# Masked softmax of variable length on one Trainium2 core: 64-byte writes beside the first loads taken out, stores of seven batches cut in halves

## The chip, the core and the metric

The kernel runs on one core of a Trainium2 chip. The time is device microseconds from launch to the end of the program, as the median of three runs. The profile is one execution of the same program; its span, from the first instruction to the last, is about 1.65 us shorter than the time of the run.

A core has engines that work side by side: VectorE (DVE), ScalarE (ACT), GpSimd (POOL), TensorE (PE) and SyncE (SP). Transfers between the chip's main memory (HBM) and the on-chip memory (SBUF, 128 partitions) are carried by 16 DMA engines. An engine's program only issues a transfer; the transfer raises a semaphore when it has landed, and other engines wait for that semaphore.

## The reference

`x` is 16 batches of 8 heads of 256 x 256 numbers in fp32, and `lengths` holds one length for each batch. Each row gets a softmax over its first `length` columns, and zeros behind it:

```python
for b in range(batch):
    length = lengths[b]
    masked = x[b, :, :, :length]
    masked = masked - np.max(masked, axis=-1, keepdims=True)
    exp_masked = np.exp(masked)
    result[b, :, :, :length] = exp_masked / np.sum(exp_masked, axis=-1, keepdims=True)
```

One batch is 2048 rows of 1 KB, that is 2.097 MB. The lengths of this case, in order of batch, are 188, 233, 229, 243, 195, 252, 165, 210, 222, 180, 209, 157, 159, 199, 214 and 248. All 16 batches are written whole, 33.6 MB.

## The kernel before

A batch is one tile of 128 partitions, 16 rows of 256 numbers in each, so 16 KB in a partition. There are eight places (`slots`) for such tiles in SBUF. Half a batch is 8 rows (8 KB) in each partition, a quarter is 4 rows (4 KB).

**Loads.** SyncE issues the loads of batches 0 to 3 at once (batch 0 in two halves). GpSimd issues those of batches 4 to 15. It picks a width of 160 to 240 columns, or all 256, by the batch's length, and has two loads in flight: before it issues load `n` it waits for load `n-2` to have landed and for the store of batch `n-8` to be done.

```python
for h in range(2):
    s = slice(h * half, (h + 1) * half)
    nc.sync.dma_start(out=xt[:, 0, s], in_=x_f[0, :, s]).then_inc(s_ld[h], 16)
for b in range(1, ahead):                                   # ahead = 4
    nc.sync.dma_start(out=xt[:, b], in_=x_f[b]).then_inc(s_ld[b + 1], 16)
...
with nc.Fori(0, (batch - ahead) // 2, 1, engines=[POOL]) as q:
    for par in range(2):
        n = 2 * q + (ahead + par)
        v_len = length(POOL, word[0:1, bass.ds(2 * n, 1)])
        with nc.gpsimd.If(q >= 1):
            nc.gpsimd.wait_ge(s_sw[par], 16 * q)            # load n-2 has landed
            nc.gpsimd.wait_ge(s_st[par], 64 * q)            # store n-8 is done
        pick(v_len, bass.ds(n, 1), bass.ds(n % slots, 1), par, widths + [seq_k])
```

**The small writes.** Ahead of the loads ScalarE's own queue gets one transfer of 640 pieces of 64 bytes (16 x 40). It writes zeros into the place of the last batch in the output, which that batch's own store overwrites at the end.

```python
nc.vector.memset(touch, 0.0).then_inc(s_zero, 1)            # 16 x 40 x 16 numbers
nc.scalar.wait_ge(s_zero, 1)
out_e = out_f[batch - 1].rearrange("(e r) t k -> e (r t) k", e=16)[:, :often, :few]
nc.scalar.dma_start(out=out_e, in_=touch).then_inc(s_touch, 16)
```

**Compute.** VectorE masks a batch in place (`mask`), ScalarE takes the exponential of its 16 rows in each partition with their sums, and VectorE divides each half (`divide`). VectorE masks batch `b+1` before it divides batch `b`:

```python
for b in range(batch):
    if b == 0:
        divide(0, 0)
    if b + 1 < batch:
        mask(b + 1, slice(0, nt))       # waits for load b+1
    if b > 0:
        divide(b, 0)
    divide(b, 1)
```

**Stores.** SyncE issues them, on the queue on which it issued the first loads. How a batch is cut depends on its number: batch 0 whole, 1 to 9 in a half and two quarters, 10 and 11 in halves, 12 to 14 whole, 15 in halves. A piece waits until its half is divided; the first piece of batch `b` also waits until the store of batch `b-2` is done.

```python
def parts(b):
    if b == 0:
        cuts = [0, nt]
    elif b < 10:
        cuts = [0, half, half + quarter, nt]
    elif b < 12 or b == batch - 1:
        cuts = [0, half, nt]
    else:
        cuts = [0, nt]
    return [slice(i, j) for i, j in zip(cuts, cuts[1:])]
...
for b in range(batch):
    s_b = s_st[b % 2]
    for s in parts(b):
        nc.sync.wait_ge(s_out, 2 * b + (s.stop - 1) // half + 1)
        if b == batch - 1 and s.start == 0:
            nc.sync.wait_ge(s_touch, 16)
        if b >= 2 and s.start == 0:
            nc.sync.wait_ge(s_b, 64 * (b // 2 + 1))
        nc.sync.dma_start(
            out=out_f[b, :, s, :], in_=xt[:, b % slots, s, :]
        ).then_inc(s_b, 16 * ((s.stop - s.start) // quarter))
```

Of the kernel before, what the change touches and what calls it, by code (L numbers as in the profile page):

```python
# [9 lines left out]
F32 = mybir.dt.float32  # L10
# [10 lines left out]
def kernel(  # L21
# [6 lines left out]
    nc = tc.nc  # L28
    P = nc.NUM_PARTITIONS

    batch, heads, seq_q, seq_k = x.shape
# [7 lines left out]
    out_f = out.rearrange("b h q k -> b (h q) k").rearrange("b (p t) k -> b p t k", p=P)  # L39
# [10 lines left out]
    def parts(b):  # L50


        if b == 0:
            cuts = [0, nt]
        elif b < 10:
            cuts = [0, half, half + quarter, nt]
        elif b < 12 or b == batch - 1:
            cuts = [0, half, nt]
        else:
            cuts = [0, nt]  # L60
        return [slice(i, j) for i, j in zip(cuts, cuts[1:])]

    pool = ctx.enter_context(tc.tile_pool(name="all", bufs=1))
# [10 lines left out]
    row_sum = pool.tile([P, batch, nt], F32, name="row_sum")  # L74
    inv_sum = pool.tile([P, batch, nt], F32, name="inv_sum")
    warm = pool.tile([P, 1], F32, name="warm")
    few = 16
    often = 40
    touch = pool.tile([16, often, few], F32, name="touch")
    seed = pool.tile([1, 2], F32, name="seed")  # L80

    with tc.tile_critical(no_gpsimd_drain=True):  # L82
        sem = lambda n: ctx.enter_context(nc.semaphore(n))
        s_word = sem("s_word")
        s_ones = sem("s_ones")
        s_touch = sem("s_touch")
        s_zero = sem("s_zero")
        s_lenb = sem("s_lenb")
        s_lenf = sem("s_lenf")
        s_ld = [sem(f"s_ld{k}") for k in range(ahead + 1)]  # L90
# [18 lines left out]


        nc.scalar.dma_start(out=word64, in_=lengths[None, :]).then_inc(s_word, 16)


        nc.vector.memset(touch, 0.0).then_inc(s_zero, 1)  # L114
        nc.scalar.wait_ge(s_zero, 1)
        out_e = out_f[batch - 1].rearrange("(e r) t k -> e (r t) k", e=16)[:, :often, :few]
        nc.scalar.dma_start(out=out_e, in_=touch).then_inc(s_touch, 16)
        for h in range(2):
            s = slice(h * half, (h + 1) * half)
            nc.sync.dma_start(out=xt[:, 0, s], in_=x_f[0, :, s]).then_inc(s_ld[h], 16)  # L120
# [2 lines left out]
        for b in range(batch):  # L123
            s_b = s_st[b % 2]
            for s in parts(b):
                nc.sync.wait_ge(s_out, 2 * b + (s.stop - 1) // half + 1)
                if b == batch - 1 and s.start == 0:
                    nc.sync.wait_ge(s_touch, 16)
                if b >= 2 and s.start == 0:
                    nc.sync.wait_ge(s_b, 64 * (b // 2 + 1))  # L130
                nc.sync.dma_start(  # L131
                    out=out_f[b, :, s, :], in_=xt[:, b % slots, s, :]
                ).then_inc(s_b, 16 * ((s.stop - s.start) // quarter))
# [49 lines left out]
        def step(ins):  # L183
# [8 lines left out]
                out=down, in0=iota_i, scalar1=0.5, scalar2=-big, op0=ALU.add, op1=ALU.mult  # L192
# [7 lines left out]
                out=len_s, in0=len_f, scalar1=big, scalar2=None, op0=ALU.mult  # L200
# [56 lines left out]
        with nc.Fori(0, 2 * batch, 1, engines=[ACT]) as i:  # L257
            nc.scalar.wait_ge(s_min, i + 1)
            at = bass.ds(i % (2 * slots), 1)
            for j in range(half):  # L260
                e = x_h[:, at, j, :]
                ins = nc.scalar.activation(  # L262
                    out=e, in_=e, func=EXP, accum_out=sum_h[:, bass.ds(i, 1), j]
# [32 lines left out]
```

The softmax here doesn't subtract the row's maximum and nothing guards it: scores larger than these inputs give would overflow.

## Time and profile before

| What | Value |
|---|---|
| time, median of 3 (lowest to highest) | 156.48 us (156.45 to 156.49) |
| span of the profiled execution | 154.8 us |
| VectorE busy | 115.6 us, 75% |
| ScalarE busy | 105.2 us, 68% |
| bytes moved by DMA | 62.12 MB, 401 GB/s over the span |
| HBM read, written | 28.51 MB, 33.60 MB |
| stores issued | 18 of 512 KB, 15 of 1024 KB, 4 of 2048 KB |
| the transfer of 64-byte pieces, issue to landing | 28.0 us |

How to read it: the busy share of an engine is an average over the span. The page names the DMA queues by number: q1 is the one that SyncE issues to, q0 GpSimd's, q10 ScalarE's. A queue's share is the time that its packets took, summed over the 16 DMA engines, divided by 16 times the span or the stretch asked for. The chain of work that ended last is followed back from the end of the last compute instruction.

### The profile page before, as it was taken

The numbers are of one execution on the slowest core, as the hardware profiler recorded it, in microseconds if no ns is written. First come the engines' busy times: TensorE is split into PE (matmuls) and PEld (weight loads), VectorE is DVE, ScalarE is ACT, GpSimd is POOL, SyncE is SP. The second block draws the span as 40 slices with busy tenths as digits, with TensorE's granted clock in tenths as the row PEclk, the third lists the DMA queues.
The fourth block names the chain that finished last, engine by engine and source line by source line (L and its number), as shares of the span: only waits on it lengthen the run. The fifth ranks groups of instructions, "written<-read, shape, count | busy, mean of one in ns | idle before, by whom it ended". The sixth has DMA issues, their size and how long they took to land.

```text
span 154.8 us, 1319 instructions
## 1 busy us (share of the span) xinstructions
PE 0.2 (0%) x1; PEld 0.1 (0%) x1; DVE 115.6 (75%) x85; ACT 105.2 (68%) x514; POOL 19.0 (12%) x25
## 2 busy tenths in 40 slices
PE   0000000000000000000000000000000000000000
PEld 0000000000000000000000000000000000000000
DVE  2339999953999993986979499999894999990000
ACT  3097799992698897393978849798979397920000
POOL 4910031000220200202020020202000000000000
DMA  4999999999999999999999999999999999999993
GB/s 110 425 442 421 425 353 405 405 412 439 418 406 390 417 407 421 410 413 415 405 424 407 411 419 401 415 406 413 416 411 448 417 423 425 442 436 428 425 417 127
DMA packets 10788, 62.12 MB, mean 401 GB/s; under 512 B 1522, under 2 KB 1618, under 8 KB 7458
## 3 DMA queue, kind: packets, MB, share of 16 engines
q1 hardware_dynamic: 6048, 41.95, 65.9%
q0 software_dynamic: 4080, 20.12, 32.1%
q10 hardware_dynamic: 658, 0.04, 0.3%
q14 instruction: 2, 0.02, 0.0%
HBM read 28.51 MB, written 33.60 MB: 401 GB/s over the span
## 4 chain that ended last, share of the span: by engine, by line
DMA 71%; DVE 12%; issue 3%; SPq 2%; POOLq 1%; DVEq 0%
DMA xt<-in_x_dram 39%; DMA out_dram<-xt 32%; DVE xt L235 9%; DVE xt L208 3%; SPq L131 1%; SPq L120 1%; DVE inv_sum L232 0%; POOLq L104 0%; POOLq L143 0%; SPq L122 0%; POOLq L148 0%; POOLq L166 0%; DVEq L225 0%; POOLq L170 0%; POOLq L150 0%
## 5 line engine op out<-in xcount | busy, mean ns | idle before, releaser
L262 ACT ACTIVATE xt<-xt x256 | 102.4, 403 | 28.8 <-DVE xt L208 28.8
L235 DVE TENSOR_TENSOR xt<-xt,inv_sum 128x2048 f32<-128x2048 f32 x32 | 73.3, 2292 | 1.1
L208 DVE SCALAR_TENSOR_TENSOR xt<-down,len_s,xt 128x2048 f32<-128x2048 f32 (+1 forms) x17 | 37.8, 2224 | 19.7 <-DMA xt<-in_x_dram 19.3
L262 ACT ACTIVATION_READ_ACCUMULATOR xt<-xt x256 | 48.3, 189 | 0.0
L143 POOL DMA_DIRECT2D xt<-in_x_dram x12 | 12.8, 1066 | 91.3 <-DMA out_dram<-xt 51.4
L232 DVE RECIPROCAL inv_sum<-row_sum 128x8 f32<-128x8 f32 x32 | 6.3, 195 | 1.1 <-ACT xt L262 1.1
L162 POOL MEMSET xt<- 128x1536 f32 x4 | 5.3, 1387 | 1.1 <-DVE len_s L199 1.1
L254 ACT ACT_TABLE_LOAD x1 | 1.3, 1283 | 2.4 <-DVE touch L114 2.4
L114 DVE MEMSET touch<- 16x640 f32 x1 | 0.6, 592 | 1.3 <-SPq L82 1.3
L199 DVE TENSOR_SCALAR len_s<-len_f 128x16 f32<-128x16 f32 x1 | 0.2, 175 | 0.4 <-PE len_f L178 0.4
L154 POOL IOTA iota_i<- 128x256 int32 x1 | 0.3, 333 | 0.6 <-SPq L82 0.6
L196 DVE CAST len_b<-word 1x16 bf16<-1x16 int32 x1 | 0.2, 161 | 0.2 <-DMA word<-in_lengths_dram 0.2
L159 POOL MEMSET seed<- 1x1 f32 x2 | 0.3, 164 | 0.0
L191 DVE TENSOR_SCALAR down<-iota_i 128x256 f32<-128x256 int32 x1 | 0.2, 243 | 0.0
L254 ACT ACTIVATE warm<-const-float32-0.0 128x1 f32<-128x1 f32 x1 | 0.2, 204 | 0.0
L157 POOL MEMSET ones<- 1x128 bf16 x1 | 0.2, 195 | 0.0
L178 PE MATMUL len_f<-len_b,ones 1*128 1x16 bf16 x1 | 0.2, 168 | 2.6 <-DVE len_b L196 2.6
L280 POOL MEMSET const-float32-0.0<- 128x1 f32 x1 | 0.1, 99 | 0.3 <-issue 0.3
L178 PEld LDWEIGHTS len_f<-len_b,ones 1*128 1x128 bf16 x1 | 0.1, 101 | 2.6 <-POOL ones L157 2.6
L280 POOL MEMSET const-float32-1.0<- 128x1 f32 x1 | 0.1, 99 | 0.0
L280 POOL MEMSET const-bfloat16-1.0<- 128x1 bf16 x1 | 0.1, 99 | 0.0
L280 POOL MEMSET const-uint8-127<- 128x1 uint8 x1 | 0.1, 99 | 0.0
(1 smaller groups left out, 0.0 us busy)
## 6 DMA issues: line engine op xcount, KB each, us to landing
out_dram<-xt SPq DMA_DIRECT2D x15, 1024.0 KB
out_dram<-xt SPq DMA_DIRECT2D x18, 512.0 KB
out_dram<-xt SPq DMA_DIRECT2D x4, 2048.0 KB
xt<-in_x_dram SPq DMA_DIRECT2D x3, 2048.0 KB, 16.0
xt<-in_x_dram POOLq DMA_DIRECT2D x3, 1728.0 KB, 15.9
xt<-in_x_dram POOLq DMA_DIRECT2D x2, 2048.0 KB, 17.4
xt<-in_x_dram POOLq DMA_DIRECT2D x2, 1600.0 KB, 14.9
xt<-in_x_dram POOLq DMA_DIRECT2D x2, 1280.0 KB, 14.1
```

The lines of the kernel that those rows point to most:

```text
L114: nc.vector.memset(touch, 0.0).then_inc(s_zero, 1)
L120: nc.sync.dma_start(out=xt[:, 0, s], in_=x_f[0, :, s]).then_inc(s_ld[h], 16)
L131: nc.sync.dma_start(out=out_f[b, :, s, :], in_=xt[:, b % slots, s, :]).then_inc(s_b, 16 * ((s.stop - s.start) // quarter))
L143: nc.gpsimd.dma_start(out=xt[:, slot, :, :w], in_=x_n[:, n, :, :w]).then_inc(s_sw[par], 16)
L162: nc.gpsimd.memset(xt[:, b, :, low:], 0.0).then_inc(s_fill, 1)
L178: nc.tensor.matmul(len_f, lhsT=ones, rhs=len_b, start=True, stop=True).then_inc(s_lenf, 1)
L208: return nc.vector.scalar_tensor_tensor(out=t, in0=down[:, None, lo:hi].to_broadcast([P, s.stop - s.start, hi - lo]), scalar=len_s[:, b : ...
L232: step(nc.vector.reciprocal(out=inv_sum[:, b, s], in_=row_sum[:, b, s]))
L235: nc.vector.tensor_tensor(out=t, in0=t, in1=inv_sum[:, b, s, None].to_broadcast([P, half, seq_k]), op=ALU.mult,).then_inc(s_out, 1)
L254: nc.scalar.activation(out=warm, in_=nc.const_aps.tensor(0.0, (P, 1), F32), func=EXP)
L262: ins = nc.scalar.activation(out=e, in_=e, func=EXP, accum_out=sum_h[:, bass.ds(i, 1), j])
L280: nc = _bacc.Bacc("TRN2", target_bir_lowering=False, num_devices=1)
```

## The change

Two things are changed at once. The transfer of 64-byte pieces is taken out, with its tile, the fill of that tile and the semaphores around it. And the cuts of the stores are moved: batches 6 to 9 go in two halves instead of a half and two quarters, and batch 12 in two halves instead of whole. So the half-and-quarters form ends with batch 5, batches 6 to 12 and 15 go in halves, and 0, 13 and 14 whole. Loads, compute and all other waits stay. Large pieces need fewer packets; how a batch's store is cut also sets in what portions the store queue takes its turns beside the load queue. The small writes had been put beside the whole loads of the start, and the last store had to wait for them.

```diff
         if b == 0:
             cuts = [0, nt]
-        elif b < 10:
+        elif b < 6:
             cuts = [0, half, half + quarter, nt]
-        elif b < 12 or b == batch - 1:
+        elif b < 13 or b == batch - 1:
             cuts = [0, half, nt]
         else:
             cuts = [0, nt]
...
-    few = 16
-    often = 40
-    touch = pool.tile([16, often, few], F32, name="touch")
...
-        s_touch = sem("s_touch")
-        s_zero = sem("s_zero")
...
-        nc.vector.memset(touch, 0.0).then_inc(s_zero, 1)
-        nc.scalar.wait_ge(s_zero, 1)
-        out_e = out_f[batch - 1].rearrange("(e r) t k -> e (r t) k", e=16)[:, :often, :few]
-        nc.scalar.dma_start(out=out_e, in_=touch).then_inc(s_touch, 16)
...
-                if b == batch - 1 and s.start == 0:
-                    nc.sync.wait_ge(s_touch, 16)
```

## The prediction, made before the changed kernel was run

> **What bounds the kernel now.** I read the page's slices first, then its queues.
>
> ```profile
> DMA  4999999999999999999999999999999999999993
> GB/s 110 425 442 421 425 353 405 405 412 439 418 406 390 417 407 421 410 413 415 405 424 407 411 419 401 415 406 413 416 411 448 417 423 425 442 436 428 425 417 127
> ...
> q1 hardware_dynamic: 6048, 41.95, 65.9%
> q0 software_dynamic: 4080, 20.12, 32.1%
> q10 hardware_dynamic: 658, 0.04, 0.3%
> ```
>
> The DMA engines are full from the second slice to the last but one, while VectorE has 75% and ScalarE 68%. So the time is a lead-in, then bytes over rate, then a short tail. It can fall only if packets cost less, and it can rise only if the engines run dry somewhere. The 6048 packets of q1 are 42 transfers (37 stores, 5 loads) of 144: 128 with data and 16 for the completion. So a batch stored in a half and two quarters is 3 x 144 = 432 packets, in halves 288, whole 144.
>
> Next, how stores (q1) and loads (q0) share the engines. This is the DMA view of 81.0 to 119.9 us, which begins where batch 6's store starts and ends with load 14:
>
> ```profile
> DMA packets 3498, 16.14 MB, mean 415 GB/s; under 512 B 272, under 2 KB 320, under 8 KB 2933
> ...
> q1 hardware_dynamic: 1758, 8.64, 54.4%
> q0 software_dynamic: 1740, 7.51, 48.1%
> ```
>
> The two queues take turns packet by packet, 1758 to 1740. The bytes are not shared evenly; they follow the size of each queue's packets.
>
> Third, the issues of stores in the timeline of SyncE's queue (start, length, last column the number issued):
>
> ```profile
> 81.00 1.34 SPq L131 DMA_DIRECT2D out_dram<-xt  x3
> 90.39 1.43 SPq L131 DMA_DIRECT2D out_dram<-xt  x3
> 99.93 1.37 SPq L131 DMA_DIRECT2D out_dram<-xt  x3
> 109.65 0.88 SPq L131 DMA_DIRECT2D out_dram<-xt  x2
> 118.95 0.88 SPq L131 DMA_DIRECT2D out_dram<-xt  x2
> ...
> 138.74 0.36 SPq L131 DMA_DIRECT2D out_dram<-xt  x1
> ```
>
> Batch b is issued when batch b-2 has landed. Batches 7, 8 and 9 are issued at 81.00, 90.39 and 99.93, and 10 and 11 at 109.65 and 118.95. So batch 6 runs from 81.0 to 90.4, and batch 9 ends at 118.95: about 9.5 us a batch. Batch 14 is issued at 138.74, so it waits for the DMA.
>
> Fourth, the end, in the chain of work (start, length, what):
>
> ```profile
> 111.93 15.18 DMA xt<-in_x_dram
> 127.11 0.03 issue
> ...
> 132.28 2.29 DVE xt L235
> ...
> 137.16 2.29 DVE xt L235
> ```
>
> The last load lands at 127.11; VectorE has batch 14 divided at 134.57 (7.5 us later) and batch 15 at 139.45. But the DMA view from 127.1 to 154.0 shows this still to be stored:
>
> ```profile
> DMA packets 1052, 10.72 MB, mean 398 GB/s; under 512 B 128, under 2 KB 128, under 8 KB 128
> ...
> q1 hardware_dynamic: 1052, 10.72, 93.6%
> ```
>
> That is 10.72 / 2.097 = 5.1 batches. At the 427 GB/s of the stretch from 127 to 152 us they last 25.1 us, to 152.2, and the remaining 2.6 us of the span are landing and close. Compute done at 139.45 hides under them. This backlog is the margin that the change spends.
>
> **What the Trainium skill says.** Its page "DMA: Bandwidth & Descriptors", section "Queues, rings and completion order", says that each DMA engine goes round-robin between the queues that have work, and switches at packet boundaries. The 1758 to 1740 agrees, and my main step rests on it. The same page, "Where 436 GB/s comes from", puts the fabric's ceiling at 435 GB/s; the trace has 430 between 4 and 20 us, so pure streams have no speed to gain. Its "Specifications" say that transfers under 512 B are done as read-modify-write. The trace shows no great price for them here, as the next part works out.
>
> **The change part by part.** (1) The small writes. The DMA view of 4 to 20 us has these lines:
>
> ```profile
> q1 hardware_dynamic: 582, 6.86, 100.5%
> q10 hardware_dynamic: 451, 0.03, 1.9%
> ```
>
> 1.9% of 16 x 16 us over 451 packets is 10.8 ns each. With 640 of data and 16 of completion, 656 x 10.8 ns / 16 engines = 0.44 us off a saturated stream. VectorE's fill of the tile (0.59 us) and ScalarE's wait fall before the first load has landed, and bring nothing. The last store's wait for these writes was met at about 30 us.
>
> (2) Four batches lose their quarters. In the view of 100 to 115 us (halves and quarters) q1 takes 54.2% of 240 engine-us for 3.33 MB, or 39.1 engine-us per MB; in that of 144 to 152 us (halves only) 98.3% of 128 for 3.34 MB, 37.7. A batch would save 1.4 x 2.1 / 16 = 0.18 us, four 0.7 us. The first stretch also has loads beside it, which stretch packets, so I count half: 0.35 us.
>
> (3) Batch 12 gets 144 more packets. At 136 to 144 us (mostly whole stores) a MB costs 100.5% of 128 / 3.44 = 37.4; 0.3 x 2.1 / 16 = 0.04 us is lost. The sum of (1) to (3) is 0.75 us less DMA work.
>
> (4) What moves: the stores take a larger share. The loads 10 to 14 need the same 1740 turns after 81.0 us, and in as many turns q1 sends 1758 packets. Before, these are 1758 / 432 = 4.07 batches; now they are 1758 / 288 = 6.10. So 2.03 batches more, 4.26 MB, are stored before load 14 has landed: 4.26 MB / 0.415 = 10.3 us. Load 14 moves from 119.9 to 130.2, less 0.75, to 129.4. The last load comes 7.2 us after it, as before, at 136.6; larger packets are a little better used, so I take 136.0 against 127.1.
>
> (5) What that does to the end. At 136.0 only 5.1 - 2.0 = 3.1 batches are left: the rest of batch 12, then 13, 14 and 15. Batch 14 is stored whole and can't be issued before it is divided, 7.5 us after the last load, at 143.5. By then batch 13 has left: it is ready 7.5 us after load 14, about 136.9, its bytes begin at about 138.4 and take 4.9 us, to 143.3. An idle queue needs about 1.5 us from issue to first bytes (the first load was issued at 1.14 us, and bytes appear between 2 and 3 us). So batch 14 sends from 145.0 to 149.9, batch 15 (divided by 148.4) to 154.8, and with the 2.6 us of landing and close the span ends at 157.4, against 154.8: 2.6 us more. All earlier stores keep pace: batch 12 is divided 7.5 us after load 13, which lands at about 118.4, and its turn comes at about 128.
>
> The saving of 0.75 us is thus in the stream, and about 3 us of dry queue at the end outweigh it. I take off 0.5 us, because each moment in which the store queue waits for compute lets the loads catch up: 156.48 + 2.1 = **158.6 us**.
>
> **The rivals.** A: the margin suffices. If load 15 lands by about 132.5, then 132.5 + 7.5 + 1.5 + 9.8 + 2.6 = 153.9, which is the span before less the saving; nothing runs dry, and the time is 155.7 us. For it: full slices everywhere, and SyncE's own waits, of which 97.8 us are on earlier stores and only 25.7 us on VectorE. Against it: the count of turns puts load 15 some 3.5 us beyond that. B: the turns hold exactly, load 15 lands at 137 or later, and batch 13 too is late: 160 to 161 us. C: the small writes did good, for example by filling bubbles of the single load queue. Then the start gets slower than before by some tenths, and the time is 156.5 to 157 with the margin whole. Against it: 100.5% of q1 in the stretch with them equals the 100.5% of the pure stores at 136 to 144 us without.
>
> **Range and chances.** A is one case in five or so, C in part with it; B is about as likely. The range runs from just below A to within B: 155.5 to 160.6. Two per cent below is 153.35, more than any saving counted here, so 0.01. Two per cent above is 159.61, reached if the last load is 1 us later than I take it: 0.23. The rest, 0.76, lies within 2%.
>
> **What would show each step.** (1) q10 with about 2 packets, and load 3's landing about 0.4 us earlier. (2) q1 packets: the stores become 18 - 8 = 10 of 512 KB, 15 + 4 + 2 = 21 of 1024 KB, and 3 of 2048 KB; 39 transfers with the loads, 5616 packets. (4) Batches from 6 on land about 7.9 us apart instead of 9.5, the turns stay 1 to 1, and the last load lands near 136. (5) SyncE waits for VectorE at batches 13 and 14, and the DMA slices show a hole between 136 and 146 us. If the last load lands before 132 with full slices to the end, step 4 is wrong and A holds. If the hole is there but the time is over 160, the start of an idle queue costs more than my 1.5 us.

## The result and the profile after

The changed kernel takes 159.17 us (median of 4, 159.11 to 159.46) against 156.49 before (four runs here, three in the table above): the ratio is 1.0172, with a 95% interval of 1.0155 to 1.0190. It is slower by 2.7 us. The page of the changed kernel has these slices and queues, which answer to those shown of before:

```profile
DMA  4999999999999999999999999999999999894994
GB/s 125 437 428 441 420 308 419 414 407 434 423 404 390 419 411 421 404 417 412 407 419 423 418 412 413 413 419 410 422 420 416 421 442 418 354 403 196 403 399 200
...
q1 hardware_dynamic: 5616, 41.95, 64.8%
q0 software_dynamic: 4080, 20.12, 31.5%
...
q10 hardware_dynamic: 2, 0.00, 0.0%
```

The packets fell as the cuts say, to 5616 on q1 and 2 on q10. But the row of full slices now has a break near its end: slices 34 and 36 (from 0) carry 354 and 196 GB/s.

The DMA view from 81 to 130 us, which ends where load 14 now lands, shows how the queues share:

```profile
DMA packets 3523, 20.53 MB, mean 419 GB/s; under 512 B 273, under 2 KB 321, under 8 KB 1944
...
q1 hardware_dynamic: 1734, 12.62, 61.9%
q0 software_dynamic: 1789, 7.91, 40.2%
```

As many turns as before, again about one to one. But q1's turns now carry 12.62 MB instead of 8.64, so 6.0 batches have been stored by load 14 and not 4.1. The timeline of SyncE's queue has the stores 8.0 us apart instead of 9.5 (start, length, number issued; batches 7 to 9 with both halves, the first halves of 10 and 11, then batch 14):

```profile
82.04 0.91 SPq L118 DMA_DIRECT2D out_dram<-xt  x2
89.80 0.87 SPq L118 DMA_DIRECT2D out_dram<-xt  x2
97.83 0.93 SPq L118 DMA_DIRECT2D out_dram<-xt  x2
105.82 0.36 SPq L118 DMA_DIRECT2D out_dram<-xt  x1
113.86 0.36 SPq L118 DMA_DIRECT2D out_dram<-xt  x1
...
144.75 0.36 SPq L118 DMA_DIRECT2D out_dram<-xt  x1
```

The chain of work of the changed kernel ends so:

```profile
120.26 17.00 DMA xt<-in_x_dram
...
142.44 2.29 DVE xt L222
...
147.32 2.29 DVE xt L222
```

The last load lands at 137.26 us, 10.15 us later than before. The second division of batch 14 ends at 144.73, and the store of the whole batch is issued at 144.75. In the view of DMA by stretches (start and end, length, clock, DMA share, GB/s) the queue can be seen to run dry:

```profile
136.00:138.00 2.00, 1.00 0.61 258
138.00:140.00 2.00, 1.00 0.94 397
140.00:142.00 2.00, 1.00 1.04 442
142.00:144.00 2.00, 1.00 0.50 213
144.00:146.00 2.00, 1.00 0.31 131
```

Against the 427 GB/s of the kernel before between 127 and 152 us, these five stretches lack 338, 60, -30, 428 and 592 units of GB/s x us, together 1388, which is 3.3 us of transfer. That covers the whole loss of 2.7 us. SyncE's waits on VectorE have gone from 25.7 to 47.7 us, while those on earlier stores fell from 97.8 to 82.2.

### The profile page after: what moved, and what is told of

It is laid out like the page before. It is cut to its first block, busy times and chain, and to the rows that moved or that the text cites. A ratio compares the mean times of both kernels' runs of the same rounds, so it can differ in the third digit from the quotient of the medians.

```text
span 157.6 us, 1314 instructions
## 1 busy us (share of the span) xinstructions
PE 0.2 (0%) x1; PEld 0.1 (0%) x1; DVE 115.2 (73%) x84; ACT 105.2 (67%) x514; POOL 19.0 (12%) x25
## 3 DMA queue, kind: packets, MB, share of 16 engines
q1 hardware_dynamic: 5616, 41.95, 64.8%
## 4 chain that ended last, share of the span: by engine, by line
DMA 76%; DVE 12%; issue 3%; SPq 2%; POOLq 1%; DVEq 0%
DMA xt<-in_x_dram 55%; DMA out_dram<-xt 21%; DVE xt L222 9%; DVE xt L195 3%; SPq L118 1%; SPq L109 1%; DVE inv_sum L219 0%; POOLq L130 0%; POOLq L135 0%; POOLq L99 0%; SPq L111 0%; POOLq L157 0%; POOLq L153 0%; DVEq L212 0%; POOLq L159 0%
## 5 line engine op out<-in xcount | busy, mean ns | idle before, releaser
L249 ACT ACTIVATE xt<-xt x256 | 102.4, 402 | 39.7 <-DVE xt L195 39.7
```

The source lines that it names most:

```text
L249: ins = nc.scalar.activation(out=e, in_=e, func=EXP, accum_out=sum_h[:, bass.ds(i, 1), j])
```

## The experiments

The theory is that of the prediction: larger store packets carry more bytes in the same number of turns, so the stores run ahead and the last load comes late, and batches 13 and 14, each stored whole, then wait for compute while the DMA queue is empty. Rivals are that the absence of the small writes costs time, that the loss is spread evenly over the batches in halves, or that the late load and its compute alone set the end. Ratios are against the kernel before, measured beside each variant, as its median differs by some tenths between sets of runs (156.49 to 156.94 us).

**Without the small writes, old cuts (e1).** The changed kernel with the old cuts:

```diff
-        elif b < 6:
+        elif b < 10:
...
-        elif b < 13 or b == batch - 1:
+        elif b < 12 or b == batch - 1:
```

> The 64-byte writes are taken out, the cuts of the stores stay as before. Theory (the writes only cost their packets, 0.44 us off a full stream): 156.0 to 156.1 us. Rival C (the writes did good at the start): the trace of the changed kernel has batch 7's store issued at 82.04 us against 81.00 before, although up to there only the writes differ; if that comes from their absence, this kernel takes 156.9 to 157.5 us.

Measured: 156.71 us, before 156.85; ratio 0.9993 (0.9980 to 1.0005). So the slowdown isn't there, and rival C falls. The gain is 0.1 us, and the interval, -0.31 to +0.08 us, leaves out the 0.44 of the prediction's step 1. The late store of batch 7 at 82.04 us doesn't come from the missing writes: here it is issued at 80.88 us, before at 81.00. GpSimd's load of batch 10 goes out at 72.49 us, before at 72.44, in the changed kernel at 72.94. In the view by stretches of 5 us, the kernel before shows

```profile
10.00:15.00 5.00, 1.00 1.01 425
15.00:20.00 5.00, 1.00 1.02 431
20.00:25.00 5.00, 1.00 1.02 352
```

and this kernel

```profile
10.00:15.00 5.00, 1.00 1.03 439
15.00:20.00 5.00, 1.00 1.00 426
20.00:25.00 5.00, 1.00 1.00 338
```

What is ahead at 15 us is gone at 25 us: over the first 25 us both have moved 9.11 MB (five rates x 5 us).

**New cuts, small writes kept (e2).** The kernel before with `b < 6` and `b < 13`:

```diff
-        elif b < 10:
+        elif b < 6:
...
-        elif b < 12 or b == batch - 1:
+        elif b < 13 or b == batch - 1:
```

> The 64-byte writes stay, the cuts are those of the changed kernel. Theory (the cuts make the loss, by a late last load and a queue that runs dry; the writes cost 0.44 us): 159.5 to 159.7 us, with the last load landing near 137.5 us. Rival C (the writes help): the cuts still lose, but less of the total is theirs: 157.9 to 158.6 us. If the cuts are innocent: about 156.5 us.

Measured: 159.31 us, ratio 1.0162 (1.0141 to 1.0184); the last load lands at 137.37 us, and the holes are there too (262 and 131 GB/s in the two stretches from 142 to 146 us). The cuts alone make the loss. The time is 0.2 us under the expected range, which counted 0.44 us for the writes.

**Only two batches changed to halves, with batch 12 (e3).**

```diff
-        elif b < 6:
+        elif b < 8:
```

> The changed kernel with the quarters kept for batches 6 and 7, so that only 8 and 9 change to halves (and 12 from whole). Turns theory: 1750 turns after batch 6 starts carry 2 x 432 and then 288 a batch, that is 2 + (1750 - 864) / 288 = 5.1 batches instead of 6.1; the last load lands 5 us earlier than in the changed kernel, at about 132.3 us, where the backlog just suffices: 155.9 to 156.9 us. Rival (the loss is spread over the batches in halves, each costing the same): half of the loss stays, 157.8 us.

Measured: 156.70 us, ratio 0.9990 (0.9976 to 1.0004); the last load lands at 132.26 us. The DMA view from 81 to 125 us, at whose end load 14 lands:

```profile
DMA packets 3507, 18.28 MB, mean 415 GB/s; under 512 B 272, under 2 KB 320, under 8 KB 2434
...
q1 hardware_dynamic: 1752, 10.68, 58.8%
q0 software_dynamic: 1755, 7.60, 43.1%
```

The same turns, 10.68 / 2.097 = 5.1 batches. The last load comes 5.15 us later than before, and this costs nothing that can be measured: from 124 to 152 us no stretch of 2 us is below 385 GB/s. The next 5.0 us, in the changed kernel, cost 2.7 us. So the loss is not spread over the batches; it begins where the backlog of stores no longer covers the last batches' compute.

**Divide before the next mask at the end (e4).** Changed kernel, with VectorE's order turned for the last batches:

```diff
-            if b + 1 < batch:
+            late = b in (13, 14)
+            if b + 1 < batch and not late:
                 mask(b + 1, slice(0, nt))
             if b > 0:
                 divide(b, 0)
             divide(b, 1)
+            if late:
+                mask(b + 1, slice(0, nt))
```

> The changed kernel, but VectorE divides batches 13 and 14 before it masks 14 and 15, so that their stores no longer wait for the load after them. Last load as in the changed kernel, 137 us. Theory (the loss is the empty DMA queue at 136 to 138 and 142 to 146 us, because batches 13 and 14 are held by the next load): the first hole vanishes and the second shrinks, 2 to 3.5 us less, 155.7 to 157.2 us. Rival (the last load itself and its 12.4 us of compute set the end, or larger store packets move fewer bytes a second): no gain, 159 us or more.

Measured: 160.88 us, ratio 1.0249 (1.0229 to 1.0269). The number is what was written for the rival, 159 us or more, but it came about in another way. VectorE's timeline (start, length, instruction, and in brackets the idle time before it) shows how:

```profile
130.83 2.34 DVE L195 SCALAR_TENSOR_TENSOR xt<-down,len_s,xt 128x2048 f32<-128x2048 f32 x1
136.75 0.20 DVE L219 RECIPROCAL inv_sum<-row_sum 128x8 f32<-128x8 f32 x1 [3.58 <-ACT xt L252]
...
142.39 2.35 DVE L195 SCALAR_TENSOR_TENSOR xt<-down,len_s,xt 128x2048 f32<-128x2048 f32 x1
```

Batch 14 is divided by 142.47, some 2.3 us earlier than in the changed kernel, as meant. But the mask of batch 15 begins at 142.39 instead of 137.50, and no longer runs beside the exponentials of batch 14; its last division ends at 154.04 instead of 149.61. The holes now lie at 140 to 144 us (369 and 238 GB/s) and behind batch 14, where the larger one is: between 148 and 150 us no packet starts, and the next 2 us have 66 GB/s. The edit changed two waits at once, so it doesn't tell the theory from its rival.

**Batches 13 and 14 in halves too (f1).** This leaves VectorE's order alone:

```diff
-        elif b < 13 or b == batch - 1:
+        elif b < batch:
```

> The changed kernel with batches 13 and 14 also stored in two halves instead of whole. The last load should land where it did, near 137 us. Theory (the holes come from batches 13 and 14 waiting, whole, for their last division): the first half of batch 14 can go at 142.3 instead of 144.75 us and that of batch 13 2.4 us earlier too, so both holes shrink by up to 2.4 us in all that is not taken back by the wait for batch 15: 157.3 to 158.3 us. Rival (the end is set by load 15 and its own compute alone): 159 us as before.

Measured: 156.76 us, before 156.54; ratio 1.0012 (1.0003 to 1.0022). The last load lands at 137.14 us, as late as in the changed kernel, and yet nearly the whole loss is gone; the rival that the late load and its compute set the end falls. The halves of batches 14 and 15 leave at 142.20, 144.63, 147.07 and 149.51 us:

```profile
142.20 0.36 SPq L118 DMA_DIRECT2D out_dram<-xt  x1
...
144.63 0.37 SPq L118 DMA_DIRECT2D out_dram<-xt  x1
...
147.07 0.37 SPq L118 DMA_DIRECT2D out_dram<-xt  x1
...
149.51 0.36 SPq L118 DMA_DIRECT2D out_dram<-xt  x1
```

One half every 2.44 us is the pace of VectorE (2.29 + 0.20, overlapping a little), and 1.05 MB at 427 GB/s is 2.46 us of transfer. From the first half on, compute feeds the queue almost exactly. What is left is mainly one dip, the stretch from 142 to 144 us at 279 GB/s:

```profile
142.00:144.00 2.00, 1.00 0.67 279
```

The expectation, 157.3 to 158.3 us, was too high by 0.5 to 1.5 us; it had set some of the gain against a wait of batch 15.

**Three times the small writes (f2).** The kernel before with `often = 120`:

```diff
-    often = 40
+    often = 120
```

> The kernel before with three times as many 64-byte writes (1920 instead of 640). Step 1 of the prediction (each costs 10.8 ns of a full engine): 2 x 0.44 = 0.9 us more, 157.7 us where the kernel before takes 156.85. Rival (most of a small write's time lies beside that of the neighbouring packets, as the run without any suggests, whose gain was 0.1 us): 0 to 0.4 us more, 156.9 to 157.2 us.

Measured: 157.28 us, before 156.54; ratio 1.0041 (1.0029 to 1.0053), so 0.45 to 0.83 us for 1280 more writes, 0.23 to 0.42 for each 640. That is nearer to the prediction's 0.44 than to the 0.1 us that taking them out brought; the intervals of the two runs meet at 0.23 to 0.31. Whether part of the gain is given back at 20 to 25 us, or the price is simply 0.25 to 0.3 us, they don't decide. Nor do they test quite the same thing: the transfer of writes now takes 59.3 us to land instead of 28.0, so many of the added writes lie beside later and smaller packets than the whole loads of the start.

**Quarters at the end (f3).** e1 with batches 12 to 14 in a half and two quarters:

```diff
-        elif b < 10:
+        elif b < 10 or 12 <= b < 15:
```

> No small writes, cuts as before, but batches 12, 13 and 14 in a half and two quarters instead of whole: they leave after the last load has landed, in a stream of stores alone, so that no share moves and only the packets count, 8 of 16 KB against 8 of 8 KB and 16 of 4 KB on each engine. Steps 2 and 3 of the prediction (0.09 to 0.18 us for a half in quarters, 0.04 for a batch in halves): 3 x 0.13 to 3 x 0.22, 0.4 to 0.7 us more than with whole stores, 157.1 to 157.4 us. Rival (packet size costs nothing in a full stream): 156.7 us.

Measured: 156.71 us, ratio 1.0015 (1.0006 to 1.0023). Against e1's 0.9993 that is 0.0022, or 0.34 us for three batches, 0.11 a batch, a little below what was expected; as the two ratios come from different sets of runs and their intervals all but meet, it is rough. The DMA view from 128 to 152 us, stores alone, has for e1

```profile
DMA packets 974, 10.26 MB, mean 427 GB/s; under 512 B 106, under 2 KB 106, under 8 KB 106
```

and for this kernel

```profile
DMA packets 1821, 10.16 MB, mean 423 GB/s; under 512 B 197, under 2 KB 197, under 8 KB 965
```

Nearly twice the packets go with 1% less rate: 0.01 x 24 us is 0.24 us, 0.08 a batch. This too is rough, as it comes from one profile of each: the two profiled executions took 156.51 us (e1) and 156.44 us.

**GpSimd's first load earlier (f4).** e1 with a wait for batch 1 instead of batch 2:

```diff
-        nc.gpsimd.wait_ge(s_ld[ahead - 1], 16)
+        nc.gpsimd.wait_ge(s_ld[ahead - 2], 16)
```

> No small writes, cuts as before, and GpSimd starts its first load when batch 1 has landed (about 13.8 us) instead of batch 2 (about 18.6 us). All kernels so far move only 315 to 352 GB/s between 20 and 25 us. If that dip is the hand-over from the loads of SyncE's queue to its stores with GpSimd's queue not yet running, it shrinks, by up to 0.9 us: 155.8 to 156.4 us. If the dip belongs to the start of GpSimd's own loads, it only moves to about 16 us: 156.7 us.

Measured: 156.65 us, ratio 1.0001 (0.9991 to 1.0012). GpSimd's first load went out at 15.91 us instead of 20.67, and 20 to 25 us still has 333 GB/s, with 424 from 15 to 20. So the dip neither shrinks nor moves; it isn't the start of GpSimd's queue. It lies where SyncE's queue passes from loads to stores, but its cause was not found.

**More quarters (g1).** Changed kernel with quarters to batch 11 and 12 whole:

```diff
-        elif b < 6:
+        elif b < 12:
...
-        elif b < 13 or b == batch - 1:
+        elif b == batch - 1:
```

> The step away from the change: no small writes, quarters for batches 1 to 11, 12 to 14 whole, 15 in halves. The turns theory puts the last load earlier: after 81 us each batch up to 11 takes 432 packets, so at load 14 the same 4.07 batches have left, and in the 7 us to load 15 fewer bytes of stores beside it: load 15 near 125 us against 127.5. The backlog grows, but a longer backlog brings nothing; two batches more with quarters cost 2 x 0.11 us (as the run with quarters at the end gave for a batch): 156.6 to 156.8 us where the kernel before takes 156.6. If an earlier last load were worth time by itself: about 2 us less, 154.6 us.

Measured: 157.04 us, before 156.94; ratio 1.0004 (0.9986 to 1.0021). No gain and no clear loss. The last load landed at 126.92 us, not near 125, so the turns theory failed here. From 119.9 us, about where load 14 lands, to 126.9 us the DMA view has 252 packets of q1 (1.14 MB) to 121 of q0 (1.72 MB); in the kernel before it has 178 (1.33 MB) to 121 from 119.9 to 127.1 us. The quarters were there, but they only got more turns. Load 15 is whole: its 121 packets, 16 of them for the completion, carry 16 KB each, while those of loads 10 to 14 carry 4.3 KB on average (7.51 MB in 1740). Beside such large load packets the turns are not one to one, in the kernel before as little as here; why, no run here shows.

**The version that the runs point to (g2).** Quarters to batch 6, halves from 7 to the end:

```diff
-        elif b < 6:
+        elif b < 7:
...
-        elif b < 13 or b == batch - 1:
+        elif b < batch:
```

> The version that the runs point to: no small writes, quarters for batches 1 to 6, halves for all of 7 to 15. Turns theory: one batch fewer in front of the last load than in the changed kernel minus a half, so it lands near 135 us; the halves of batches 13 and 14 leave as soon as they are divided, so no hole is left. Packets saved against the cuts of before: 3 x 0.11 for quarters, less 3 x 0.04 for halves instead of whole, with 0.1 for the small writes 0.3 us: 156.2 to 156.4 us where the kernel before takes 156.6. If the packet savings aren't real: 156.6 to 156.8 us.

Measured: 156.74 us, before 156.94; ratio 0.9985 (0.9973 to 0.9997). The last load lands at 134.51 us, later than whole stores of batches 13 and 14 could bear by the estimate of rival A (132.5 us), and from 134 us on no stretch of 2 us up to 150 us is below 414 GB/s. It is faster than the kernel before by about 0.2 us (0.05 to 0.4), and so than the changed kernel by some 2.9 us. With the queue full to the end, what is won is about the 0.3 us expected of fewer packets and no small writes, and no more.

## Why the prediction was right

The time was forecast as 158.6 us, and is 159.17.

The turns (step 4) held up to load 14: one to one, 6.0 batches instead of the forecast 6.1 at load 14, 8.0 us between batches for 7.9. The last load came at 137.26 us for 136.0; the uncut count had given 136.6, and the profiled run was 1.04 us behind the one before at batch 7 already (82.04 against 81.00), which e1, with the same cuts up to there and no writes either, was not (80.88). The 7.2 us from load 14 to load 15, taken over from before, came out as 7.3, though turns do not explain them: from 130.0 to 137.2 us q1 has 202 packets to 105 of q0. The store pieces beside load 15 are of 8 KB in both kernels, and so the stretch stayed the same.

The end (step 5) held in kind: holes in the DMA at 136 to 138 and 142 to 146 us, one for each of the batches 13 and 14, and batch 14 issued 7.5 us after the last load. Its parts were off in both directions. An idle queue sends sooner than the 1.5 us estimated: batch 14, issued at 144.75, has its first packets in the quarter of a microsecond from 145.50, and batch 13, issued at 137.41, from 138.25, so 0.75 to 1.1 us. From the last packets, at about 155.4, to the span's end it took 2.2 us and not 2.6. With these, 137.3 + 7.5 + 0.8 + 9.8 + 2.2 = 157.6, the measured span. That the forecast came so near is in part luck: the last load was 1.3 us later than it took, and the start of the idle queue and the tail together 1.1 us shorter. By its own reckoning, a last load 1 us later would have meant 159.61 us.

The savings were the terms that were mis-sized. For the small writes 0.44 us was put; taking them out brought 0.1 (-0.08 to 0.31). Load 3, which was to land 0.4 us earlier, landed no earlier: at about 24.3 us before (issued at 3.6, 20.7 us to landing) and 24.7 after (3.3 and 21.4). The packets' durations were summed as if each stood alone on a full engine, though q1 and q10 had 102.4% between them in that stretch. A part may have lain beside other packets, but this was not shown. For quarters against halves 0.35 us was put for four batches; f3 gives 0.08 to 0.11 for a batch against whole stores, of which 0.04 was counted for halves, so roughly 0.2 to 0.3 for four. The 0.5 us taken off for loads catching up has no counterpart: the sum without it, 2.6 us, is nearly the measured 2.7.

Of the rivals, A failed on this kernel and is what happens in e3, where the last load lands at 132.26, just inside the 132.5 us that A needed, though without A's saving: it takes 156.70 us, where A said 155.7. B had the last load right, at 137 or later, but not the time: batch 13 was late, but its bytes were through at about 143 us, ahead of the issue of batch 14 at 144.75, so that added nothing to the end. C failed in e1.

## What to carry to other kernels

Where two DMA queues stay full, packet size bears on how they share the engines: before making one stream's transfers larger, count in turns what this does to the arrival of the other, and check in the trace that the turns are one to one (they were for loads in packets of about 4 KB, and not for the one in packets of 16 KB). A stream that is ahead costs nothing until the backlog at the end is shorter than the compute behind the last arrival; then cut the last pieces so that each leaves as soon as it is ready, for that gave back 2.5 of 2.7 us with the last load as late as ever. Fewer packets say little by themselves: in a stream of stores alone, nearly half the packets went with 1% more rate.

## What was not expected of the hardware

A 64-byte write beside packets of 4 to 16 KB costs little: 1280 of them on 16 engines took 0.45 to 0.83 us, 6 to 10 ns each. And all variants move only 315 to 360 GB/s between 20 and 25 us, where the whole loads of the start give way to stores, while the share of the DMA engines stays at 0.95 to 1.02; an earlier start of the other load queue did not change it.
